# A decoder trunk on one core: operands and weights at one distance modulo 256 bytes, and a few pieces of weights 128 bytes off

## The chip, the cores and the metric

One Trainium2 chip, one of its cores. The metric is the device time of one execution in microseconds (us); a run of the kernel before takes 2272.42 us, the median of three (2271.67 to 2273.33). One further execution was profiled, and its rows are read below.

## What is computed

Two layers of a hybrid decoder on 256 tokens, model width 2048, all float32. Each layer is

```python
h = rms_norm(x, norm1_w)
proj = h @ w_in                                  # 2048 -> 6400
ret = retention(heads(rq), heads(rk), heads(rv), pos)          # 6 heads x 128
att = dilated_attention(heads(aq), heads(ak), heads(av))       # 6 heads x 128
gm  = chunk_gmlp(gu, gv, gmlp_ln_w, gmlp_ws, gmlp_bs)          # 4 groups x 128
mixed = concat(silu(rg) * norm(ret), norm(att), norm(gm))
x = x + mixed @ w_out                            # 2048 -> 2048
x = x + conv_ffn(rms_norm(x, norm2_w), w_up, conv_w, conv_b, w_down)   # 2048 -> 2 * 5632 -> 2048
```

and a last RMS norm follows. Nearly all the work is in the four weight matrices, which are read once each: 792 pieces of 128 x 1024 floats.

## The kernel before

The activations stay in SBUF; the weights come as one stream of pieces, 128 partitions x 1024 floats (4 KB in a partition, 512 KB in all). A piece is loaded into a `raw` buffer by SP, then cut into two float32r tiles: `hi` by ScalarE (line 113) and `lo = raw - hi` by VectorE (line 123), four buffers each. An operand is cut in the same way and lies as one tile of 2 x 256 columns, its high part first: `p0` to `p15` hold the normalised input of a layer half (line 266), `q0` to `q15` what goes into `w_out` (the mixers' outputs) and into `w_down` (the gated up-projection). A product of two floats is then three float32r matmuls of 256 columns: hi by high part, hi by low part, lo by high part. So each piece, eight blocks of 128 x 128, is 24 matmuls, in both forms of the projection:

- `proj_t` (matmul at line 355): the weights are the stationary operand, and `p` or `q` streams past. It does the attention's and the retention's q and k, `w_out`, `w_up` and `w_down`.
- `proj_n` (line 395): here `p` is the stationary operand, and a stretch of `hi` or `lo` streams past. It does the values and gates of the mixers (token major).

By layer the pieces are: attention q and k (24 pieces), attention v (12, `proj_n`), retention q and k (24), then 40 pieces of `proj_n`, `w_out` (32), and three parts of the feed-forward, each `w_up` and then `w_down`: 64 and 32, 64 and 32, 48 and 24. Layer 0 is pieces 0 to 395, layer 1 is 396 to 791.

Between the pieces stand the small matmuls in plain float32: the sums of the norm (lines 310 and 320), the heads of attention and retention (434, 435, 457 to 459, 489, 490, 499 to 501), the gating (554) and the transposes (420, 450). The order is written out by hand: `take` steps the queues of small work (`ev`, `bg`) at each new piece and splits the piece that is three ahead.

Where a tile lies follows from the order of the pools and the tiles' sizes. In the built program the sixteen `p` tiles lie at 192 modulo 256 bytes, and every `hi` and `lo` at 0. The `q` tiles come from `q_tile` (line 412), which makes each one 112 floats longer than its 512 and starts at one of eight places in it:

```python
STARTS = [b // 4 for b in (0, 128, 320, 384, 448, 64, 192, 256)]

def q_tile(slot, which):
    a = STARTS[which]
    return qp.tile([P, 2 * S + 112], F32R, name=f"q{slot}", tag=f"q{slot}")[:, a : a + 2 * S]
```

A `q` tile is therefore 2496 bytes, 9 x 256 + 192, and neighbours lie 192 bytes apart modulo 256: the streaming operand goes round 192, 128, 64 and 0 modulo 256 within every piece of `w_out` and `w_down`. The blocks of one piece start 512 bytes apart, the high and low part of an operand 1024 bytes, so neither changes the place modulo 256. The 128-byte tile `shim` in a pool of its own (line 167, 220) does nothing but move what follows it.

Of the kernel before, what the change touches and what calls it, by code (L numbers as in the profile page):

```python
# [41 lines left out]

PIECE = 1024
PPC = 1
RAW = 4
CHUNK = PIECE * PPC
TOTAL = DEPTH * (D * INW + D * D + D * UPW + DFF * D) // P
NCHUNK = TOTAL // CHUNK
FFN_PARTS = ((0, 16), (16, 32), (32, 44))


# [16 lines left out]
Q_ATT, Q_GM, Q_RET = 0, 6, 10  # L68


class Weights:


    def __init__(self, nc, stream, raw, hp, lp, ahead, step):
        self.nc, self.stream, self.raw, self.hp, self.lp = nc, stream, raw, hp, lp
        self.ahead, self.step = ahead, step
        self.plan = []
        self.pos = 0
        self.loaded = {}
        self.nload = 0  # L80
        self.parts = {}
        self.nsplit = 0
        self.npieces = TOTAL // PIECE

    def load(self, upto):
        while self.nload < min(upto, NCHUNK):
# [16 lines left out]
    def split_hi(self, p, halves=(0, 1)):  # L103
        c = p // PPC
        self.load(c + 1)
        src = self.loaded[c][:, (p % PPC) * PIECE : (p % PPC + 1) * PIECE]
        if p not in self.parts:
            hi = self.hp.tile([P, PIECE], F32R, name=f"hi{p}", tag="hi")
            lo = self.lp.tile([P, PIECE], F32R, name=f"lo{p}", tag="lo")
            self.parts[p] = (hi, lo, src)  # L110
        hi = self.parts[p][0]
        for h in self._halves(p, halves):
            self.nc.scalar.activation(hi[:, h], src[:, h], AF.Copy)  # L113
# [40 lines left out]
def trunk_kernel(tc, x0, xt, stream, par, cst, wst, lnw, out):  # L154
# [5 lines left out]
    with ctx:  # L160
        E = ctx.enter_context

        def pool(name, bufs=1):
            return E(tc.tile_pool(name=name, bufs=bufs))

        cp, xp, pp, qp = pool("cst"), pool("xres"), pool("px"), pool("qx")
        gap = pool("gap")
        wk, fw = pool("mix"), pool("ffn")
        raw, hp, lp = pool("raw", RAW), pool("hi", 4), pool("lo", 4)
        ps = E(tc.tile_pool(name="ps", bufs=4, space=bass.MemoryType.PSUM))  # L170
# [32 lines left out]
        W = Weights(nc, stream, raw, hp, lp, 3, step)  # L203
        live = [0]

        def mm():
            until(lambda: live[0] < 4)
            live[0] += 1
            return ps.tile([P, 512], F32, name="mm", tag="mm")
# [7 lines left out]

        prm = cp.tile([P, NPAR], F32, name="prm")
        warm = cp.tile([P, 2], F32, name="warm")
        shim = gap.tile([P, 32], F32, name="shim")  # L220
        GP.memset(shim, 0.0)
        GP.memset(warm, 0.0)
        A.activation(warm, warm, AF.Copy)
        first = xp.tile([P, NK + 4 * S], F32, name="xg0", tag="xg0")
# [77 lines left out]
        def finish_norm(rot, final=False):  # L302
            while norm["n"] < NK:
                yield
            for _ in range(0 if final else 4 if W.pos < 10 * PIECE else 2):
                yield
            t = mx()
            for j in range(2):
                for i, part in enumerate((norm["acc"], norm["end"])):
                    T.matmul(t[:, j : j + 1], part[:, j * P : (j + 1) * P], ones[:, 0:1], start=i == 0, stop=i == 1)  # L310
            ms = cp.tile([P, 2], F32, name="ms", tag="ms")
            rcol = cp.tile([P, 2], F32, name="rcol", tag="rcol")
            V.tensor_scalar(ms, t[:, 0:2], 1.0 / D, EPS, op0=ALU.mult, op1=ALU.add)
            GP.tensor_tensor(rcol, ms, mhalf[:, 0:2], op=ALU.pow)
            diag = cp.tile([P, S], F32, name="diag", tag="diag")
            for j in range(2):
                V.tensor_scalar(diag[:, j * P : (j + 1) * P], ident, rcol[:, j : j + 1], None, op0=ALU.mult)
            yield
            t = mx()
            T.matmul(t[:, 0:S], ones, diag, start=True, stop=True)  # L320
            if final:
                rbc = t[:, 0:S]
            else:
                rbc = cp.tile([P, S], F32, name="rbc", tag="rbc")
                A.activation(rbc, t[:, 0:S], AF.Copy)
            norm["col"], norm["bc"] = rcol, rbc
            norm["ready"] = True
            if rot:
                for _ in range(12):
                    yield  # L330
                c = wk.tile([P, S], F32, name="cosr", tag="cosr")
                s = wk.tile([P, S], F32, name="sinr", tag="sinr")
# [73 lines left out]
            until(lambda: QX[k] is not None)  # L406
            return QX[k]


        STARTS = [b // 4 for b in (0, 128, 320, 384, 448, 64, 192, 256)]  # L410

        def q_tile(slot, which):
            a = STARTS[which]
            return qp.tile([P, 2 * S + 112], F32R, name=f"q{slot}", tag=f"q{slot}")[:, a : a + 2 * S]

        def mixed_block(slot, l, src, c0):

            t = mx()
            for j in range(2):
                T.transpose(t[:, j * P : (j + 1) * P], src[j][:, c0 : c0 + P], ident)  # L420
            q = q_tile(slot, 4 * l)
            w = prm[:, C_MIX + l * NK + slot : C_MIX + l * NK + slot + 1]
            yield
            split_hi(q, t[:, 0:S], w)
            split_lo(q, t[:, 0:S], w)
            QX[slot] = q


        def attention(h, qk, av, done):
            for _ in range(h if h < WIDTH else 0):  # L430
                yield
            t = mx()
            q, k = qk[h][:, 0:S], qk[h][:, S : 2 * S]
            T.matmul(t[:, 0:P], q[:, 0:P], k[:, 0:P], start=True, stop=True)  # L434
            T.matmul(t[:, P : 3 * P], q[:, P : 2 * P], k, start=True, stop=True)  # L435
            yield
            s = wk.tile([P, 384], F32, name="s", tag="s", bufs=3)
            V.scalar_tensor_tensor(s, t[:, 0:384], SCALE, LC, op0=ALU.mult, op1=ALU.add)
            nm = wk.tile([P, 2], F32, name="nm", tag="nm", bufs=3)
            V.tensor_reduce(nm[:, 0:1], s[:, 0:P], axis=AX.X, op=ALU.max, negate=True)  # L440
            V.tensor_reduce(nm[:, 1:2], s[:, P:384], axis=AX.X, op=ALU.max, negate=True)
            yield
            den = wk.tile([P, 2], F32, name="den", tag="den", bufs=3)
            A.activation(s[:, 0:P], s[:, 0:P], AF.Exp, bias=nm[:, 0:1], accum_out=den[:, 0:1])
            A.activation(s[:, P:384], s[:, P:384], AF.Exp, bias=nm[:, 1:2], accum_out=den[:, 1:2])
            yield
            V.reciprocal(den, den)
            t = mx()
            for i in range(3):
                T.transpose(t[:, i * P : (i + 1) * P], s[:, i * P : (i + 1) * P], ident)  # L450
# [6 lines left out]
            T.matmul(t[:, 0:P], pt[:, 0:P], av[0][:, c], start=True, stop=True)  # L457
            T.matmul(t[:, P : 2 * P], pt[:, P : 2 * P], av[0][:, c], start=True, stop=False)  # L458
            T.matmul(t[:, P : 2 * P], pt[:, 2 * P : 384], av[1][:, c], start=False, stop=True)  # L459
# [26 lines left out]
        def retention(h, qk, rv, scale):  # L486
            t = mx()
            q, k = qk[h][:, 0:S], qk[h][:, S : 2 * S]
            T.matmul(t[:, 0:S], k[:, 0:P], q, start=True, stop=True)  # L489
            T.matmul(t[:, S : S + P], k[:, P : 2 * P], q[:, P : 2 * P], start=True, stop=True)  # L490
# [5 lines left out]
            yield  # L496
            c = slice(h * P, (h + 1) * P)
            t = mx()
            T.matmul(t[:, 0:P], s[:, 0:P], rv[0][:, c], start=True, stop=True)  # L499
            T.matmul(t[:, P : 2 * P], s[:, P : 2 * P], rv[0][:, c], start=True, stop=False)  # L500
            T.matmul(t[:, P : 2 * P], s[:, 2 * P : 384], rv[1][:, c], start=False, stop=True)  # L501
            yield
            for j in range(2):
                V.tensor_copy(rv[j][:, c], t[:, j * P : (j + 1) * P])
# [41 lines left out]
        def gmlp(l, gu, gv, ws, done):  # L546
# [3 lines left out]
            for j in range(2):  # L550
                t = mx()
                for g in range(G):
                    c = slice(g * P, (g + 1) * P)
                    T.matmul(t[:, c], ws[:, c], gv[j][:, c], start=True, stop=True)  # L554
                yield
                for g in range(G):
                    c = slice(g * P, (g + 1) * P)
# [58 lines left out]
        for l in range(DEPTH):  # L616
# [92 lines left out]
            hsn, an = [0], [0]  # L709
            A_TAGS = ("gu0", "gu1", "gv0", "gv1")  # L710

            def up_evac(f0, part):
                gate = {}

                def ev_up(m, acc):
# [16 lines left out]
                        return  # L732
                    V.tensor_tensor(a, a, gate.pop(f), op=ALU.mult)  # L733
                    yield
                    q = q_tile(f - f0, part)
                    A.activation(q[:, 0:S], a, AF.Copy)  # L736
                    yield
                    V.tensor_tensor(q[:, S : 2 * S], a, q[:, 0:S].bitcast(F32), op=ALU.subtract)
# [3 lines left out]
            for i, (f0, f1) in enumerate(FFN_PARTS):  # L742
                last = i == len(FFN_PARTS) - 1
                QX[:] = [None] * NK
                cols = [c for f in range(f0, f1) for c in (f * P, DFF + f * P)]
                proj_t("w_up", l, allrows, cols, p_of, up_evac(f0, 4 * l + 1 + i), 4)
                wcol = None
                if last:
                    PX[:] = [None] * NK
# [100 lines left out]
```

## Time and profile before

| | |
|---|---|
| median of three runs | 2272.42 us |
| the profiled execution | 2269.97 us |
| its span, first to last instruction | 2268.2 us |
| TensorE busy in the span | 2251.2 us, 19430 matmuls |
| VectorE, ScalarE, GpSimd busy | 1443.3, 1143.5, 21.8 us |
| data moved | 425 MB, 187 GB/s on average |
| granted TensorE clock, mean | 0.998 |

The profile counts a matmul as busy from its start to a modelled end, and neighbours overlap, so "99% busy" does not say how fast matmuls follow each other. That is read by dividing a stretch of time by the number of matmuls that start in it. In the view of the chain, which follows the work that ended last, consecutive matmuls of one line are merged into one row with their time and their count, and the quotient stands there directly; a row that begins right behind other matmuls leaves its first one out.

### The profile page before, as it was taken

To read this page: it belongs to the slowest core of one execution; us is meant where nothing else is said; L and a number is where in the kernel's file an instruction comes from. 1 tells how busy PE (TensorE), PEld (TensorE's weight loads), DVE (VectorE), ACT (ScalarE), POOL (GpSimd) and SP (SyncE) were. 2 spreads that over 40 slices of the span, in tenths; PEclk is the share of its full clock that TensorE was granted. 3 is DMA by queue.
4 is the path that set the end of the run, shared out by engine and by line. 5 is a ranking of instruction groups with operands and counts; after the bars stand their busy time and mean duration, and the time that the engine had idled before them with its cause. 6 is when DMAs were issued, how large, how long until landed. Compare 5 with 4: busy or idle time off the path is not lost.

```text
span 2268.2 us, 45995 instructions
## 1 busy us (share of the span) xinstructions
PE 2251.2 (99%) x19430; PEld 2248.1 (99%) x19430; DVE 1443.3 (64%) x2086; ACT 1143.5 (50%) x1616; POOL 21.8 (1%) x39
## 2 busy tenths in 40 slices
PE   9999999999999999999999999999999999999997
PEld 8999999999999999999999999999999999999997
DVE  6565556677547775577655655667775577656765
ACT  6475554555435553455544644555554355434553
POOL 0000000000000000000000001000000000000000
PEclk9999999999999999999999999999999999999999
DMA  8545445555555555565555454555555555555553
GB/s 283 193 158 187 160 168 194 188 194 195 186 186 196 195 182 197 179 206 189 184 201 180 164 180 168 178 184 192 193 192 188 185 199 193 194 186 189 193 191 126
DMA packets 117135, 425.15 MB, mean 187 GB/s; under 512 B 12992, under 2 KB 12992, under 8 KB 116800
## 3 DMA queue, kind: packets, MB, share of 16 engines
q1 hardware_dynamic: 116928, 422.21, 54.8%
q8 instruction: 152, 2.49, 0.4%
q14 instruction: 55, 0.45, 0.1%
HBM read 420.06 MB, written 2.10 MB: 186 GB/s over the span
## 4 chain that ended last, share of the span: by engine, by line
PE 99%; DMA 0%; DVE 0%; SPq 0%; ACT 0%; POOLq 0%; issue 0%; DVEq 0%
PE mm L355 84%; PE mm L395 13%; PE mx L420 0%; DMA xg<-in_xt_dram 0%; PE mx L435 0%; PE mx L489 0%; DVE xg L760 0%; PE mx L310 0%; PE mx L450 0%; PE mx L554 0%; PE mx L458 0%; PE mx L500 0%; PE mx L459 0%; PE mx L501 0%; PE mx L499 0%; PE mx L434 0%
## 5 line engine op out<-in xcount | busy, mean ns | idle before, releaser
L123 DVE TENSOR_TENSOR lo<-raw,hi 128x1024 fp32r<-128x1024 f32 (+1 forms) x793 | 969.0, 1223 | 710.4 <-ACT hi L113 710.2
L113 ACT ACTIVATE hi<-raw 128x1024 fp32r<-128x1024 f32 (+1 forms) x793 | 837.5, 1058 | 881.8 <-PE mm L355 490.7
L355 PE MATMUL mm<-p,hi 128*128 128x256 f32 x7168 | 1235.4, 277 | 5.5 <-ACT hi L113 5.2
L355 PEld LDWEIGHTS mm<-p,hi 128*128 128x128 f32 x7168 | 1084.6, 188 | 6.9 <-ACT hi L113 5.2
L355 PE MATMUL mm<-p,lo 128*128 128x256 f32 x3584 | 991.8, 277 | 0.0
L355 PE MATMUL mm<-q,hi 128*128 128x256 f32 x3840 | 684.8, 281 | 0.0
L355 PEld LDWEIGHTS mm<-p,lo 128*128 128x128 f32 x3584 | 674.3, 188 | 0.5 <-DVE lo L123 0.2
L355 PEld LDWEIGHTS mm<-q,hi 128*128 128x128 f32 x3840 | 589.3, 188 | 0.0
L355 PE MATMUL mm<-q,lo 128*128 128x256 f32 x1920 | 538.4, 280 | 0.0
L355 PEld LDWEIGHTS mm<-q,lo 128*128 128x128 f32 x1920 | 361.6, 188 | 0.0
L395 PE MATMUL mm<-hi,p 128*128 128x256 f32 x1664 | 272.1, 279 | 0.0
L395 PEld LDWEIGHTS mm<-hi,p 128*128 128x128 f32 x1664 | 231.2, 188 | 0.0
L395 PE MATMUL mm<-lo,p 128*128 128x256 f32 x832 | 179.3, 278 | 0.0
L724 ACT ACTIVATE a<-hs,prm 128x256 f32<-128x256 f32 x176 | 104.1, 591 | 63.3 <-DVE hs L369 63.3
L395 PEld LDWEIGHTS mm<-lo,p 128*128 128x128 f32 x832 | 133.3, 188 | 0.0
L727 DVE SCALAR_TENSOR_TENSOR a<-hs,prm,a 128x256 f32<-128x256 f32 x176 | 85.3, 485 | 6.3
L726 DVE SCALAR_TENSOR_TENSOR a<-hs,prm,a 128x256 f32<-128x256 f32 x176 | 84.2, 478 | 4.4 <-ACT a L724 4.4
L692 DVE TENSOR_TENSOR xg<-xg,mm 128x256 f32<-128x256 f32 x128 | 53.3, 418 | 50.7 <-PE mm L355 50.7
L369 DVE TENSOR_TENSOR hs<-mm,rbc 128x256 f32<-128x256 f32 x176 | 73.5, 418 | 2.7 <-PE mm L355 2.7
L730 ACT ACTIVATE a<-a 128x256 f32<-128x256 f32 x88 | 35.6, 405 | 33.5 <-DVE a L727 33.5
L279 ACT ACTIVATE t<-xg 128x256 f32<-128x256 f32 x75 | 30.1, 408 | 39.9 <-DVE xg L692 38.9
L736 ACT ACTIVATE q<-a 128x256 fp32r<-128x256 f32 x88 | 35.4, 403 | 3.5 <-DVE a L733 3.5
(120 smaller groups left out, 578.4 us busy)
## 6 DMA issues: line engine op xcount, KB each, us to landing
raw<-in_stream_dram SPq DMA_DIRECT2D x791, 512.0 KB, 3.4
out_dram<-xg SPq DMA_DIRECT2D x8, 256.0 KB, 2.4
xg<-in_xt_dram SPq DMA_DIRECT2D x3, 512.0 KB, 8.6
cs<-in_cst_dram SPq DMA_DIRECT2D x1, 1216.0 KB, 8.7
raw<-in_stream_dram SPq DMA_DIRECT2D x2, 256.0 KB, 4.2
ws<-in_wst_dram SPq DMA_DIRECT2D x2, 256.0 KB, 4.5
lw<-in_lnw_dram SPq DMA_DIRECT2D x2, 256.0 KB, 4.7
prm<-in_par_dram SPq DMA_DIRECT2D x1, 412.0 KB, 6.0
```

The costliest lines, as they stand in the source:

```text
L113: self.nc.scalar.activation(hi[:, h], src[:, h], AF.Copy)
L123: self.nc.vector.tensor_tensor(lo[:, h], src[:, h], hi[:, h].bitcast(F32), op=ALU.subtract)
L279: A.activation(sq, X[j], AF.Square)
L355: T.matmul(acc[m], w, v, start=k == 0 and i == 0, stop=k == n - 1 and i == 2)
L369: V.tensor_tensor(out, acc, norm["bc"], op=ALU.mult)
L395: T.matmul(acc[j][:, c], v, w[:, c], start=k == 0 and i == 0 and c.start == 0, stop=k == NK - 1 and i == 2, skip_group_check=True)
L692: V.tensor_tensor(X[m], X[m], acc, op=ALU.add)
L724: A.activation(a, hs[:, 2 : S + 2], AF.Identity, scale=conv_col(ch, 2), bias=conv_col(ch, 3))
L726: V.scalar_tensor_tensor(a, hs[:, 1 : S + 1], conv_col(ch, 1), a, op0=ALU.mult, op1=ALU.add)
L727: V.scalar_tensor_tensor(a, hs[:, 0:S], conv_col(ch, 0), a, op0=ALU.mult, op1=ALU.add)
L730: A.activation(a, a, AF.Silu)
L736: A.activation(q[:, 0:S], a, AF.Copy)
```

## The change

It touches where tiles lie, and nothing of what is computed. Four things change:

1. `q_tile` with its eight starts is gone, and with it the padding: a `q` tile has 512 floats, 2048 bytes, as a `p` tile has. So all `q` tiles lie at 192 modulo 256, where the `p` tiles lie.
2. `hi` and `lo` tiles get 64 floats more (`SLACK`), and a piece starts 32 floats into them if it goes to `proj_t` and 0 floats if it goes to `proj_n` (`PLACES`, `token_major`). With `shim` removed the tiles' own start moves as well: in the built program a piece of `proj_t` lies at 0 modulo 256, 192 bytes before its operand, and a piece of `proj_n` at 128, which is 192 past the operand at 192 (before: at 0, which is 64 past it).
3. Every small float32 matmul and transpose sets a mark (`stirred`). The next piece that gets its buffers then starts at the other of the two places and clears the mark, if at least four pieces (`APART`) have gone since the last such one. Its distance is then 64 bytes and not 192. In the built program these are 40 pieces, 20 in each layer: 10, 14, 39, 43, 47, 51, 55, 59, 63, 75, 79, 83, 87, 91, 95, 99, 103, 107, 137 and 141 in layer 0; 401, 405, and then 396 past those from 39 on in layer 1.
4. There are five `raw` buffers in place of four.

```diff
-RAW = 4
+RAW = 5
+SLACK = 64
+PLACES = ((32, 0), (0, 32))
+APART = 4
...
+def token_major(p):
+    p %= LAYER_PIECES
+    a, b = QK_PIECES + AV_PIECES, 2 * QK_PIECES + AV_PIECES
+    return QK_PIECES <= p < a or b <= p < b + REST_PIECES
...
+    def place(self, p):
+        other = self.stirred and p - self.moved >= APART
+        if other:
+            self.stirred, self.moved = False, p
+        a = PLACES[token_major(p)][other]
+        return slice(a, a + PIECE)
...
         if p not in self.parts:
-            hi = self.hp.tile([P, PIECE], F32R, name=f"hi{p}", tag="hi")
-            lo = self.lp.tile([P, PIECE], F32R, name=f"lo{p}", tag="lo")
-            self.parts[p] = (hi, lo, src)
+            at = self.place(p)
+            hi = self.hp.tile([P, PIECE + SLACK], F32R, name=f"hi{p}", tag="hi")
+            lo = self.lp.tile([P, PIECE + SLACK], F32R, name=f"lo{p}", tag="lo")
+            self.parts[p] = (hi[:, at], lo[:, at], src)
...
+        def matmul(*args, **kw):
+            W.stirred = True
+            T.matmul(*args, **kw)
+
+        def transpose(*args):
+            W.stirred = True
+            T.transpose(*args)
...
-        shim = gap.tile([P, 32], F32, name="shim")
-        GP.memset(shim, 0.0)
...
-            q = q_tile(slot, 4 * l)
+            q = qp.tile([P, 2 * S], F32R, name=f"q{slot}", tag=f"q{slot}")
...
-                    q = q_tile(f - f0, part)
+                    q = qp.tile([P, 2 * S], F32R, name=f"q{f - f0}", tag=f"q{f - f0}")
```

All the small matmuls and transposes now go through `matmul` and `transpose`, so a profile of the changed kernel shows them under the lines of these two helpers.

TensorE, ScalarE and VectorE get the same instructions in the same order as before, and GpSimd loses the fill of `shim`. What moves is on SP, by the fifth buffer. At the start of the program (the rows carry the tile that is loaded, its number, and the events that the load waits for), the loads of the weights stood so:

```order
L232 DMA xg3_99<-in_xt_dram 128x1024 [waits DMAHW1_49]
L89 DMA raw4_211<-in_stream_dram 128x1024 [waits DMAHW3_49,DMAHW2_49,DVE_49]
L89 DMA raw5_213<-in_stream_dram 128x1024 [waits DMAHW5_49,DVE_49]
L89 DMA raw6_215<-in_stream_dram 128x1024 [waits DMAHW6_49,DMAHW4_49,DVE_49]
L89 DMA raw7_221<-in_stream_dram 128x1024 [waits DMAHW7_49,DVE_49]
```

and now:

```order
L265 DMA xg3_94<-in_xt_dram 128x1024 [waits DMAHW1_49]
L115 DMA raw4_206<-in_stream_dram 128x1024 [waits DMAHW2_49]
L115 DMA raw5_208<-in_stream_dram 128x1024 [waits DMAHW3_49,DVE_49]
L115 DMA raw6_210<-in_stream_dram 128x1024 [waits DMAHW5_49,DMAHW4_49,DVE_49]
L115 DMA raw7_212<-in_stream_dram 128x1024 [waits DMAHW6_49,DVE_49]
```

The load of piece 4 no longer waits for VectorE, which had to be done with piece 0 in the same buffer; each later one waits for a split that comes one piece earlier. A little further on, the tables (`cs`: masks and rotation; `prm`: scales and convolution) stood among the loads so:

```order
L89 DMA raw13_465<-in_stream_dram 128x1024
L597 DMA cs_114<-in_cst_dram 128x2432
L89 DMA raw14_514<-in_stream_dram 128x1024
L89 DMA raw15_520<-in_stream_dram 128x1024
L89 DMA raw16_554<-in_stream_dram 128x1024
L600 DMA prm_90<-in_par_dram 128x824
```

and now:

```order
L115 DMA raw14_462<-in_stream_dram 128x1024
L623 DMA cs_109<-in_cst_dram 128x2432
L115 DMA raw15_511<-in_stream_dram 128x1024
L115 DMA raw16_517<-in_stream_dram 128x1024
L115 DMA raw17_551<-in_stream_dram 128x1024
L626 DMA prm_87<-in_par_dram 128x824
```

Each table stands behind one more load of weights than before.

## Rows read from the trace of the kernel before

**Rows 1.** The page: busy time by engine; the chain's shares by line.

```profile
PE 2251.2 (99%) x19430; PEld 2248.1 (99%) x19430; DVE 1443.3 (64%) x2086; ACT 1143.5 (50%) x1616; POOL 21.8 (1%) x39
...
PE mm L355 84%; PE mm L395 13%; PE mx L420 0%; DMA xg<-in_xt_dram 0%; PE mx L435 0%; PE mx L489 0%; DVE xg L760 0%; PE mx L310 0%; PE mx L450 0%; PE mx L554 0%; PE mx L458 0%; PE mx L500 0%; PE mx L459 0%; PE mx L501 0%; PE mx L499 0%; PE mx L434 0%
```

**Rows 2.** Stretches, TensorE: length, busy time (matmuls), granted clock, DMA share, GB/s.

```profile
322.31:402.10 79.79, 79.79 (x674) 1.00 0.54 183
414.44:577.64 163.20, 163.20 (x1442) 1.00 0.56 192
577.64:668.95 91.31, 91.31 (x770) 1.00 0.56 189
668.95:843.06 174.11, 174.11 (x1538) 1.00 0.57 192
843.06:933.98 90.92, 90.92 (x771) 1.00 0.56 189
...
1064.54:1133.06 68.52, 68.52 (x578) 1.00 0.55 191
1444.96:1524.52 79.56, 79.56 (x675) 1.00 0.54 182
...
1700.05:1790.96 90.91, 90.91 (x770) 1.00 0.55 190
...
1965.05:2055.97 90.92, 90.92 (x770) 1.00 0.57 190
...
2186.53:2254.93 68.40, 68.40 (x578) 1.00 0.43 146
```

**Rows 3.** The chain from 60 to 330: start, length, engine and line, instructions.

```profile
77.28 32.64 PE mm L395 x288
...
110.57 2.74 PE mm L355 x24
...
113.96 2.84 PE mm L355 x24
...
187.32 32.64 PE mm L395 x288
...
229.58 14.14 PE mm L395 x120
...
304.50 5.66 PE mm L395 x48
```

**Rows 4.** The chain of the whole span: around the norm between the layers.

```profile
1139.47 2.93 PE mm L355 x24
1142.40 0.43 PE mx L320 x2
1142.83 57.14 PE mm L355 x504
```

**Rows 5.** Instructions in order, TensorE: the end of `w_down`, the start of `w_up`.

```profile
933.62 0.40 PE L355 MATMUL mm<-q,hi 128*128 128x256 f32 x2
...
933.98 0.40 PE L355 MATMUL mm<-p,hi 128*128 128x256 f32 x2
...
934.32 0.39 PE L355 MATMUL mm<-p,hi 128*128 128x256 f32 x2
934.55 0.28 PE L355 MATMUL mm<-p,lo 128*128 128x256 f32 x1
```

**Rows 6.** The page: the splits' busy and idle time; then loads, last us to landing.

```profile
L113 ACT ACTIVATE hi<-raw 128x1024 fp32r<-128x1024 f32 (+1 forms) x793 | 837.5, 1058 | 881.8 <-PE mm L355 490.7
...
raw<-in_stream_dram SPq DMA_DIRECT2D x791, 512.0 KB, 3.4
```

**Rows 7.** The table `cs`: its first reader, and its load (min/median/max, first and last start).

```profile
L333 DVE TENSOR_TENSOR cosr<-cs,rbc x2: 419/420/420, 68.6 to 1175.0; 128x256 f32<-128x256 f32 x2
...
L597 SPq DMA_DIRECT2D cs<-in_cst_dram x1: 426/426/426, 32.2 to 32.2; - x1
```

More of the change, by code (lines that the diff above doesn't have):

```diff
@@ L48 @@
 NCHUNK = TOTAL // CHUNK
+SLACK = 64
+PLACES = ((32, 0), (0, 32))
+LAYER_PIECES = TOTAL // PIECE // DEPTH
+QK_PIECES = 2 * H * D // PIECE
+AV_PIECES = H * D // PIECE
+REST_PIECES = (2 * H + 2 * G) * D // PIECE
+APART = 4
 FFN_PARTS = ((0, 16), (16, 32), (32, 44))
@@ L83, in __init__ @@
         self.npieces = TOTAL // PIECE
+        self.stirred = False
+        self.moved = 0
+    def place(self, p):
[4 more added lines that the diff above has]
+        return slice(a, a + PIECE)
     def load(self, upto):
@@ L166, in trunk_kernel @@
         cp, xp, pp, qp = pool("cst"), pool("xres"), pool("px"), pool("qx")
-        gap = pool("gap")
         wk, fw = pool("mix"), pool("ffn")
@@ L309, in finish_norm @@
                 for i, part in enumerate((norm["acc"], norm["end"])):
-                    T.matmul(t[:, j : j + 1], part[:, j * P : (j + 1) * P], ones[:, 0:1], start=i == 0, stop=i == 1)
+                    matmul(t[:, j : j + 1], part[:, j * P : (j + 1) * P], ones[:, 0:1], start=i == 0, stop=i == 1)
             ms = cp.tile([P, 2], F32, name="ms", tag="ms")
@@ L319, in finish_norm @@
             t = mx()
-            T.matmul(t[:, 0:S], ones, diag, start=True, stop=True)
+            matmul(t[:, 0:S], ones, diag, start=True, stop=True)
             if final:
@@ L407, in q_of @@
             return QX[k]
[L410 to L414, printed above, removed]
         def mixed_block(slot, l, src, c0):
@@ L419, in mixed_block @@
             for j in range(2):
-                T.transpose(t[:, j * P : (j + 1) * P], src[j][:, c0 : c0 + P], ident)
-            q = q_tile(slot, 4 * l)
+                transpose(t[:, j * P : (j + 1) * P], src[j][:, c0 : c0 + P], ident)
+            q = qp.tile([P, 2 * S], F32R, name=f"q{slot}", tag=f"q{slot}")
             w = prm[:, C_MIX + l * NK + slot : C_MIX + l * NK + slot + 1]
@@ L433, in attention @@
             q, k = qk[h][:, 0:S], qk[h][:, S : 2 * S]
-            T.matmul(t[:, 0:P], q[:, 0:P], k[:, 0:P], start=True, stop=True)
-            T.matmul(t[:, P : 3 * P], q[:, P : 2 * P], k, start=True, stop=True)
+            matmul(t[:, 0:P], q[:, 0:P], k[:, 0:P], start=True, stop=True)
+            matmul(t[:, P : 3 * P], q[:, P : 2 * P], k, start=True, stop=True)
             yield
@@ L449, in attention @@
             for i in range(3):
-                T.transpose(t[:, i * P : (i + 1) * P], s[:, i * P : (i + 1) * P], ident)
+                transpose(t[:, i * P : (i + 1) * P], s[:, i * P : (i + 1) * P], ident)
             yield
@@ L456, in attention @@
             t = mx()
-            T.matmul(t[:, 0:P], pt[:, 0:P], av[0][:, c], start=True, stop=True)
-            T.matmul(t[:, P : 2 * P], pt[:, P : 2 * P], av[0][:, c], start=True, stop=False)
-            T.matmul(t[:, P : 2 * P], pt[:, 2 * P : 384], av[1][:, c], start=False, stop=True)
+            matmul(t[:, 0:P], pt[:, 0:P], av[0][:, c], start=True, stop=True)
+            matmul(t[:, P : 2 * P], pt[:, P : 2 * P], av[0][:, c], start=True, stop=False)
+            matmul(t[:, P : 2 * P], pt[:, 2 * P : 384], av[1][:, c], start=False, stop=True)
             yield
@@ L488, in retention @@
             q, k = qk[h][:, 0:S], qk[h][:, S : 2 * S]
-            T.matmul(t[:, 0:S], k[:, 0:P], q, start=True, stop=True)
-            T.matmul(t[:, S : S + P], k[:, P : 2 * P], q[:, P : 2 * P], start=True, stop=True)
+            matmul(t[:, 0:S], k[:, 0:P], q, start=True, stop=True)
+            matmul(t[:, S : S + P], k[:, P : 2 * P], q[:, P : 2 * P], start=True, stop=True)
             yield
@@ L498, in retention @@
             t = mx()
-            T.matmul(t[:, 0:P], s[:, 0:P], rv[0][:, c], start=True, stop=True)
-            T.matmul(t[:, P : 2 * P], s[:, P : 2 * P], rv[0][:, c], start=True, stop=False)
-            T.matmul(t[:, P : 2 * P], s[:, 2 * P : 384], rv[1][:, c], start=False, stop=True)
+            matmul(t[:, 0:P], s[:, 0:P], rv[0][:, c], start=True, stop=True)
+            matmul(t[:, P : 2 * P], s[:, P : 2 * P], rv[0][:, c], start=True, stop=False)
+            matmul(t[:, P : 2 * P], s[:, 2 * P : 384], rv[1][:, c], start=False, stop=True)
             yield
@@ L553, in gmlp @@
                     c = slice(g * P, (g + 1) * P)
-                    T.matmul(t[:, c], ws[:, c], gv[j][:, c], start=True, stop=True)
+                    matmul(t[:, c], ws[:, c], gv[j][:, c], start=True, stop=True)
                 yield
@@ L710, in trunk_kernel, with up_evac @@
             A_TAGS = ("gu0", "gu1", "gv0", "gv1")
-            def up_evac(f0, part):
+            def up_evac(f0):
                 gate = {}
@@ L745, in trunk_kernel @@
                 cols = [c for f in range(f0, f1) for c in (f * P, DFF + f * P)]
-                proj_t("w_up", l, allrows, cols, p_of, up_evac(f0, 4 * l + 1 + i), 4)
+                proj_t("w_up", l, allrows, cols, p_of, up_evac(f0), 4)
                 wcol = None
```

## The prediction, made before the changed kernel ran

> **What bounds the kernel now.** First the page: TensorE is busy 99% of the span, and the chain of work that ended last lies with 84% on line 355 and 13% on line 395, the two projections [rows 1]. Everything else is beside them, so only what changes the spacing of those matmuls can change the time by much. Busy time hides the spacing; the next view is therefore stretches of single stages, each cut at the start of its first matmul. A stretch counts one to three matmuls too many, those that reach over its ends; the real number is pieces times 24.
>
> In `w_up` the 60 pieces from 414.44 take 163.20 us for 1440 matmuls, 113.33 ns each, and the 64 from 668.95 take 174.11 for 1536, 113.35. The `w_down` between them, from 577.64, takes 91.31 for 768: 118.89. The others: 90.92, 90.91 and 90.92 for 768 each (118.4), 68.52 and 68.40 for 576 (119.0 and 118.8). `w_out` without its first four pieces: 79.79 and 79.56 for 672 (118.7 and 118.4) [rows 2]. The same instruction, the same clock of 1.00, the same share of DMA, and 5.3 ns apart. What differs is the place of the streaming operand: `p` always at 192 past the weights modulo 256, `q` going round four places.
>
> The third view, the chain, shows that the place is not all. With `p` as operand throughout, a piece behind attention's float32 matmuls runs 24 matmuls in 2.74 us (114) or in 2.84 (118). In `proj_n` the first 288 take 32.64 (113.3), twice; behind the retention's matmuls 120 take 14.14 (117.83), and this stays so up to 48 in 5.66 at 304.50: ten such stretches, 28 pieces in each layer [rows 3]. So at one distance there are two paces, 113.33 and 117.83, and small float32 work can put TensorE from the first into the second. It also comes back: behind the norm's line 310 a piece takes 2.93 us, and behind line 320 the next 504 take 57.14, 113.4 [rows 4]. I call these fast and slow. One piece at the slow pace costs 24 x 4.50 = 0.108 us.
>
> **The other views that bear on this change.** Coming from the mixed places onto `p` ended fast all seven times: the two long `w_up` stretches of rows 2 begin right behind `w_out` or `w_down`. In two of the seven the last `q` stood at 64, the distance of the moved pieces: there three matmuls at 64 start 0.36 us before the next three, and from 934.32 the step is down to about 0.34 [rows 5]. This is the nearest row for what a moved piece does.
>
> **The change part by part.** All sums are against the profiled execution, 2269.97 us with a span of 2268.2; it is 2.45 under the median of the runs, to which I add the result at the end.
>
> *`q` at 192 in `w_down`.* The operands then lie as `p` lies in the `w_up` before, with no float32 work between, so the pace is carried over. The six stretches sum to 500.98 us for 4224 matmuls [rows 2]; at 113.33 they take 478.71. Gain 22.27.
>
> *`q` at 192 in `w_out`.* The two stretches of 28 pieces sum to 159.35 for 1344 [rows 2]; fast they take 152.32, gain 7.03. It begins behind transposes, so it needs the moved piece just before it (103, 499) to leave it fast. A moved piece (107, 503) lies in each, slow by my estimate below: 0.22. Net 6.82. The first four pieces I leave as they are.
>
> *The moved pieces themselves.* The trace has whole pieces at 64 only in `proj_n`: fast at 32.64 for 288, slow at 14.14 for 120 [rows 3]. In the mixed `w_down` the three matmuls at 64 take 0.36 [rows 5], so about slow. From 0 to 0.108 us each; I take 0.108, since the row at line 355 is nearer to them than `proj_n`.
>
> *`proj_n`, now at 192.* Of the 28 slow pieces of a layer I count fast only those between a moved piece and the next float32 work: 76 to 78, 80, 84, 85, 88, 92 to 94 and 96, eleven. Piece 63, fast now, becomes a moved one. Net ten pieces, 1.08 us a layer, 2.16 in all.
>
> *Retention's q and k.* Pieces 47, 51 and 59 are fast and get moved, 39 is half; 56 becomes fast. Net 0.27 a layer, a loss of 0.54. The heads' `q` and `k` tiles move to 192 as well. The piece behind a head that already lay there takes 2.74 us (at 110.57), that behind the next head 2.84 (at 113.96) [rows 3]; this could give three pieces a layer. I leave that gain of up to 0.65 to the range.
>
> *Moved pieces in fast stretches.* 10 and 14, 137 and 141, and the same four in layer 1: 8 x 0.108 = 0.86 lost.
>
> *The fifth `raw` buffer.* A load lands in 3.4 us, and the split on ScalarE is idle 490.7 us waiting for TensorE to free a `hi` buffer [rows 6]: weights are never late, so deeper loading gains nothing behind the start. On SP, `cs` is now behind one more load. It is issued at 32.2 and first read at 68.6 [rows 7]; 3.4 later is still early. `prm` is behind one load more as well, and is read later still. The load of piece 4 no longer waits for VectorE and may run beside the last loads of `x`; that delays the start by anything from 0 to the 3.4 of one load. I take 0, since pieces 1 to 3 go ahead of it already, and keep 3.4 for the range. If this cover went, ScalarE's split would be late first and the matmuls at line 355 behind it.
>
> *Removed fill of `shim`, wider tiles.* GpSimd is busy 21.8 us of the span [rows 1], and the splits process as many elements as before. Nothing.
>
> The sum: 22.27 + 6.82 + 2.16 - 0.54 - 0.86 = 29.85. The profiled execution would be 2240.1, and the median 2272.42 - 29.85 = **2242.6 us**. A measurement of this kernel tells about 0.2%, 4.5 us, from no change.
>
> **A rule that speaks against it.** The rows say that the spacing follows the operand's place [rows 2]. The Trainium skill says otherwise: its page "TensorE: Matmul & The Clock Gate", section "Step-by-step: what each phase is for", gives TensorE two independent read ports to SBUF, one for the streaming operand and one for the weights, and says that loading the next weights takes no read bandwidth from the running matmul. By that rule the sum is 0 and the time 2272.4. The trace differs: 118.89 against 113.33 ns.
>
> **The rivals.**
>
> *A: places do not matter (4%).* Something else that `w_out` and `w_down` share sets their pace, such as the residual adds or the order of `q`. For it: the trace has no long run of `q` at 192. Against it: `proj_n` slows to almost the same pace with `p`, and with none of that work. Gain 0, or the small losses above: 2272 to 2274.
>
> *B: a moved piece does not restore the fast pace (13%).* Then `w_out` runs slow at 117.83, 158.36 for the two stretches, a gain of 0.99; `proj_n` gains nothing and loses piece 63, 0.22; retention loses three moved pieces a layer, 0.65, and the fast stretches 0.86. With `w_down`, which does not depend on it, 22.27 + 0.99 - 0.22 - 0.65 - 0.86 = 21.53: **2250.9**. For it: 64 to 192 shows only behind three matmuls at 64, with the operand moved and not the weights.
>
> *C: moved pieces end in the slow pace (7%), slower than before.* The place is behind 137 and 141: from there to the end of the layer some 258 pieces have no float32 work that could put it right. In each layer these, about 25 behind 10 and 14, 12 behind 59, the 27 of `w_out` and the 11 of `proj_n` would cost 0.108 more than forecast: 333 x 0.108 = 36.0, in both 71.9, so **2314**. It decides when some 276 pieces that I count at 113.33 ns take 117.83 (29.85 / 0.108); a single bad landing behind 141 costs 27.9 and all but eats the gain. Against it: seven fast landings of seven.
>
> *D: at 192 `proj_n` finds back by itself, and moved pieces are as fast as the others (15%).* For it: at line 355, at 192, pieces behind float32 work are often fast; at line 395, at 64, none of the ten stretches is. Then 38 moved pieces that I charge cost nothing (4.1), nine unmoved pieces a layer of `proj_n` turn fast (1.9), and the heads give 0.65: **2236**.
>
> **How the numbers follow.** My forecast has 61%, D 15%, B 13%, C 7%, A 4%. The range goes from D's 2236 to B's 2251; inside it lies the 3.4 of a late start. It leaves out C and A. Faster by over 0.2%: forecast, B, D and the mildest of C, 0.90. Within 0.2%: A and a C with one bad landing, 0.04. Slower: 0.06.
>
> **What would show it.** In the changed profile, stretches of `w_down` at 113.3 ns a matmul, 87.04 us for 32 pieces, show the first term; anything near 118 is A. `w_out` behind piece 107 at 113.3 shows that a moved piece restores, 117.8 is B. A `w_up` behind piece 141 at 117.8 is C. A moved piece takes 2.83 us if I price it rightly, 2.72 in D. The first matmul at 5.2 us as before, and ScalarE still waiting for TensorE, show that the fifth buffer is neutral. I am wrong if `w_down` is not uniform, or if its pace depends on more than the distance modulo 256.

## The result and the profile after

The changed kernel takes 2241.84 us (median of four runs, 2241.59 to 2242.37); the kernel before, run beside it on that chip, 2272.05 (2270.55 to 2273.33). The ratio is 0.9868 with a 95% interval of 0.985 to 0.9885: faster, by more than the 0.2% that can be told. On another chip the two stood at 2242.03 and 2270.09, a ratio of 0.9876 (0.9861 to 0.9891). The forecast was 2242.6 with a range of 2236 to 2251.

The profiled executions are 2269.97 us before and 2242.37 after, 27.6 apart, against a forecast of 29.85. That the forecast of the median came within 0.8 is in part luck: the runs of before that it started from lay some 2 us above those of the other chip, where the gain is 28.06.

The page of the changed kernel, its busy time, the chain's shares, the splits and the loads:

```profile
PE 2223.4 (99%) x19430; PEld 2220.2 (99%) x19430; DVE 1443.3 (64%) x2086; ACT 1143.9 (51%) x1616; POOL 24.4 (1%) x38
...
PE mm L388 84%; PE mm L428 13%; PE mx L235 2%; PE mx L239 0%; DMA xg<-in_xt_dram 0%; DVE xg L786 0%; SPq L125 0%; SPq L261 0%; POOLq L870 0%; DVEq L870 0%; ACT p L290 0%; DVE diag L350 0%; DVE xg L718 0%; ACT t L312 0%; DVE ms L346 0%
...
L140 ACT ACTIVATE hi<-raw 128x1024 fp32r<-128x1024 f32 (+1 forms) x793 | 837.4, 1058 | 851.3 <-PE mm L388 459.5
...
raw<-in_stream_dram SPq DMA_DIRECT2D x791, 512.0 KB, 3.8
```

Against [rows 1] and [rows 6] nothing has changed places: the same 19430 matmuls, TensorE at 99%, the chain with 84 and 13% on the two projections (now lines 388 and 428), the split still waiting for TensorE. TensorE's busy time fell by 27.8 us: the same work is spaced more tightly. So the stretches again, cut at the first matmul of a stage as in [rows 2] (length, busy time and matmuls, granted clock, DMA share, GB/s). In the order shown: the moved piece 103; pieces 104 to 106; the moved piece 107; 108 to 131; then `w_up` and `w_down` in turn, and three stretches of layer 1.

```profile
320.04:322.96 2.92, 2.92 (x28) 1.00 0.52 180
322.96:331.12 8.16, 8.16 (x75) 1.00 0.45 152
331.12:333.84 2.72, 2.72 (x27) 1.00 0.34 133
333.84:399.12 65.28, 65.28 (x579) 1.00 0.59 197
...
411.45:574.65 163.20, 163.20 (x1442) 1.00 0.60 192
574.65:661.69 87.04, 87.04 (x771) 1.00 0.58 198
661.69:835.77 174.08, 174.08 (x1539) 1.00 0.57 192
835.77:922.81 87.04, 87.04 (x771) 1.00 0.58 199
...
1053.37:1118.65 65.28, 65.28 (x579) 1.00 0.58 200
...
1431.10:1507.26 76.16, 76.16 (x674) 1.00 0.56 189
1682.80:1769.83 87.03, 87.03 (x770) 1.00 0.57 198
```

`w_down` takes 87.04 us for 768 matmuls, 113.33 ns each, exactly the number that the prediction asked for; `w_out` from piece 104 on takes 8.16 + 2.72 + 65.28 = 76.16 for 28 pieces, 113.33 too. A moved piece inside a stretch of the fast pace (107) takes 2.72, no more than its neighbours. The clock is 1.00 and the DMA share what it was.

The chain from 60 to 420 (start, length, engine and line, instructions) shows what was lost:

```profile
77.40 33.92 PE mm L428 x288
111.32 0.66 PE mx L235 x4
111.98 2.74 PE mm L388 x24
114.71 0.66 PE mx L235 x4
115.37 2.74 PE mm L388 x24
...
134.95 1.32 PE mx L235 x10
136.28 2.82 PE mm L388 x24
...
188.50 33.08 PE mm L428 x288
...
231.21 13.73 PE mm L428 x120
...
253.80 14.14 PE mm L428 x120
...
296.30 5.66 PE mm L428 x48
...
320.29 84.43 PE mm L388 x744
404.72 0.79 PE mx L235 x8
405.51 2.93 PE mm L388 x24
408.44 0.43 PE mx L235 x2
```

In [rows 3] the first 288 matmuls of `proj_n` took 32.64, twice. Now the first such stretch takes 33.92, 117.8 ns each, and the second 33.08: pieces 60 to 63 are slow in it. Nothing in the prediction allowed for that. The piece behind a head that was slow at 113.96 in [rows 3] now takes 2.74 (at 115.37).

### The profile page after: what moved, and what is told of

Same layout as the page of the kernel before. It is cut to its first block, busy times and chain, and to the rows that moved or that the text cites. A ratio compares the mean times of both kernels' runs of the same rounds, so it can differ in the third digit from the quotient of the medians.

```text
span 2240.6 us, 45994 instructions
## 1 busy us (share of the span) xinstructions
PE 2223.4 (99%) x19430; PEld 2220.2 (99%) x19430; DVE 1443.3 (64%) x2086; ACT 1143.9 (51%) x1616; POOL 24.4 (1%) x38
## 4 chain that ended last, share of the span: by engine, by line
PE 99%; DMA 0%; DVE 0%; SPq 0%; ACT 0%; POOLq 0%; issue 0%; DVEq 0%
PE mm L388 84%; PE mm L428 13%; PE mx L235 2%; PE mx L239 0%; DMA xg<-in_xt_dram 0%; DVE xg L786 0%; SPq L125 0%; SPq L261 0%; POOLq L870 0%; DVEq L870 0%; ACT p L290 0%; DVE diag L350 0%; DVE xg L718 0%; ACT t L312 0%; DVE ms L346 0%
## 5 line engine op out<-in xcount | busy, mean ns | idle before, releaser
L140 ACT ACTIVATE hi<-raw 128x1024 fp32r<-128x1024 f32 (+1 forms) x793 | 837.4, 1058 | 851.3 <-PE mm L388 459.5
L388 PE MATMUL mm<-q,hi 128*128 128x256 f32 x3840 | 655.2, 276 | 0.0
L388 PEld LDWEIGHTS mm<-q,hi 128*128 128x128 f32 x3840 | 578.6, 188 | 0.0
L388 PE MATMUL mm<-q,lo 128*128 128x256 f32 x1920 | 530.1, 276 | 0.0
```

The costliest lines, as they stand in the source:

```text
L388: T.matmul(acc[m], w, v, start=k == 0 and i == 0, stop=k == n - 1 and i == 2)
```

## The experiments

Two questions stood: which of the forecast's terms carried the gain, and what made 2.25 us less of it. The theory: distance sets the paces, a moved piece restores the fast one, and `proj_n` at 192 loses at its first piece. The rivals: moved pieces do nothing here, the places themselves do all (or: distance does not matter, only the order of the work). A border is the change from one form of the projection to the other; a landing is the step from a moved piece back to the usual distance. Every kernel here computes all that the reference does; only addresses and the number of buffers differ. Times are medians; where there is one run its time stands.

**1. No moved pieces.**

```diff
-        a = PLACES[token_major(p)][other]
+        a = PLACES[token_major(p)][0]
```

> The changed kernel with no piece moved: every piece of weights stays at its usual place, 192 from its operand. Theory (TensorE has two paces, 113.3 and 117.8 ns a matmul; float32 work can put it into the slow one, and a step of the distance from 64 to 192 takes it back): w_out runs at 117.8 from its first pieces to the norm's matmuls, 85.5 us for 30 pieces against 81.6 now, pieces 64 to 71 and 460 to 467 stay slow (0.86 us a layer), and so do 76 to 78, 80 and 88 and their like; w_down keeps 113.3. Together 4.7 us a layer, about 2251.8. Rival (the distance alone sets the pace, the moved pieces are idle): no stage changes, 2242.4.

Measured: 2242.66 us (2241.19 to 2243.16), ratio 0.9878 (0.9863 to 0.9893). The rival's number, but not its reason: the stages did change, and what they lost and won cancels. The chain of this kernel:

```profile
76.72 33.92 PE mm L428 x288
...
187.65 33.92 PE mm L428 x288
...
231.20 13.62 PE mm L428 x120
...
296.16 5.46 PE mm L428 x48
...
319.75 84.35 PE mm L388 x744
```

`w_out` runs at 113.4 ns (84.35 for 744) with no moved piece in it: piece 103 left the transposes ahead of it in the fast pace. The second 288 of `proj_n` are slow throughout, 33.92 against 33.08 after; this is what the moved piece 63 had bought, pieces 64 to 71. Piece 80 was bought as well. The moves cost as much: pieces 40, 55, 75, 87, 95, 96, 97, 99 and 103 are fast here and slow in the changed kernel (74 to 78 take 13.62 here and 13.73 there, 95 and 96 take 5.46 and 5.66). That is nine pieces a layer against nine, so that the sum stays is luck.

**2. `proj_n` at 64 again, moved pieces kept.**

```diff
-PLACES = ((32, 0), (0, 32))
+PLACES = ((32, 0), (32, 0))
```

> The changed kernel with the two places of proj_n exchanged: the usual distance is 64 again, as in the kernel before, and a moved piece is at 192. Theory (the twelve pieces of attention's v and the first of the gates are slow now because the border from proj_t to proj_n at 192 puts TensorE into the slow pace, and at 64 it does not): pieces 24 to 35 and 60 to 62 run at 113.3 again, 1.28 + 0.32 us a layer, so about 2239.2, if a step from 192 back to 64 restores as often as one from 64 to 192 does now. If that step never restores, five later pieces a layer turn slow, 0.54: 2240.3. Rival (the slow start of proj_n has another cause, such as the wider tiles or the fifth buffer): 24 to 35 stay at 117.8 and the time stays at 2242.4.

Measured: 2241.53 us (2241.33 to 2241.9), ratio 0.9874 (0.9857 to 0.989). The chain:

```profile
77.75 32.64 PE mm L428 x288
...
187.57 33.60 PE mm L428 x288
```

The first 288 are back at 113.3, so `proj_n`'s new distance is what made its beginning slow, and not the wider tiles or the fifth buffer. The second lost 0.96: the moved piece 63, at 192 among pieces at 64, is slow itself, and the pieces behind it stay slow. Landings from 192 on 64 spoil there: three a layer were entered fast, and the piece behind was slow each time (80, 84 and 96). With pieces 63 to 71 slow and these landings, the time lies above both of the theory's numbers, 2239.2 and 2240.3.

**3. `q` at 192 alone: `proj_n` at 64, no moved pieces.**

```diff
-        a = PLACES[token_major(p)][other]
+        a = 32
```

> The q tiles at 192 and nothing else: no piece moved, proj_n at 64 as in the kernel before. Theory: w_down 113.3 in all six stretches, pieces 24 to 35 and 60 to 71 at 113.3 as in the kernel before, the 28 pieces of proj_n behind the retention at 117.8, w_out at 117.8 up to the norm: about 2247, so about five sixths of the gain. Rival (the moved pieces bring nothing, and proj_n at 64 is better than at 192): at or under 2242.

Measured: 2245.88 us (2244.97 to 2249.13), ratio 0.9896 (0.9881 to 0.991). The theory's number, about 1 under it. The chain:

```profile
77.05 32.64 PE mm L428 x288
...
318.52 87.63 PE mm L388 x744
```

Here `w_out` runs at 117.8 ns from end to end, 3.2 us lost a layer, though its own operands lie exactly as in experiment 1. The two kernels differ in the distance of `proj_n` alone, so what ran before `w_out` decides.

**4. Four `raw` buffers.**

```diff
-RAW = 5
+RAW = 4
```

> The changed kernel with four raw buffers. Theory (weights are never late): the time of the changed kernel within 0.5 us, 2242; the first two pieces within 0.4 us of the kernel before. Rival (five buffers carry part of the gain): over 2244, with waits of ScalarE's split for loads.

Measured: 2243.95 us in one run. The time is 2 over the theory's and just under the rival's; the split waits once for a load, 0.8 us (once, 0.4, in the changed kernel). Every stage behind the first has the excess of the changed kernel, to 0.01 us (the excess is defined in the next section); the 1.68 lies ahead of `proj_n`:

```profile
2.66 6.45 DMA xg<-in_xt_dram
...
9.69 24.41 PE mm L388 x180
...
79.08 33.92 PE mm L428 x288
```

In the changed kernel these rows read 5.86, 23.33 and a start at 77.40. Of the 1.68, 0.64 is the pace of pieces 2 to 7, which run at 117.8 here. They do so too in the second execution of the changed kernel, which has five buffers and starts `proj_n` at 78.17. The first load of `x` took from 5.28 to 7.04 us with five buffers (experiments 1 and 5) and 5.70 in experiment 8 with four. `proj_n` starts at 77.28 before (four buffers), at 77.13 in experiment 8 (four) and at 78.47 in experiment 5 (five). The start varies by as much, and one run does not settle what the fifth buffer is worth.

**5. `proj_n` at 64 where it is entered from `proj_t`, at 192 behind float32 work; moved pieces in `proj_t` alone.**

```diff
+def early(p):
+    p %= LAYER_PIECES
+    return p < QK_PIECES + AV_PIECES or 2 * QK_PIECES + AV_PIECES <= p < 2 * QK_PIECES + 2 * AV_PIECES
...
+        if token_major(p):
+            a = 32 if early(p) else 0
+            return slice(a, a + PIECE)
```

> proj_n at 64 for the 24 pieces of a layer that follow proj_t without float32 work (24 to 35, 60 to 71), at 192 for the 28 behind the retention, no moved piece in proj_n; proj_t moved as in the changed kernel. Theory (a border from proj_t keeps the pace at 64 and loses it at 192; behind float32 work 192 finds back now and then, 64 almost never): the 24 run at 113.3 (2.72 us a piece), the 28 as in the run without moved pieces (about 1.6 us a layer over 113.3), w_out fast from the piece behind the moved one: about 2237.5, 4 to 5 below the changed kernel. Rival (the paces behind float32 work are a toss that any shift throws anew): the 24 fast, the 28 anything from all slow to half fast, 2236 to 2240.

Measured: 2238.42 us (2237.3 to 2240.23), ratio 0.9855 (0.9836 to 0.9874). With moved pieces in `proj_t` alone, those of `w_out` fall on 100, 104 and 108 in place of 103 and 107. It was run again beside the changed kernel on one chip:

> The kernel with two distances in proj_n once more, beside the changed kernel on one chip: 2238, 3 to 5 below the changed kernel. Rival (the difference was one of chips): under 1 apart.

> The changed kernel once more, for the comparison: 2242, excesses over 113.3 by stage as in its first profile.

Measured: 2238.58 (2238.09 to 2238.99), ratio 0.986 (0.9844 to 0.9877), against 2242.03 (2241.2 to 2242.62) of the changed kernel; before took 2270.09. The chain in the second execution:

```profile
78.10 32.64 PE mm L436 x288
...
187.92 32.64 PE mm L436 x288
...
222.52 5.46 PE mm L436 x48
229.98 14.13 PE mm L436 x120
```

Both long stretches are at 113.3. This is the best version found: 3.45 us under the changed kernel, 31.5 under the one before. 1.28 us a layer come from the first stretch, 0.65 from the later ones. The late pieces are not as in experiment 1, as the theory had them: 72 and 73 are fast here and slow there, 74 to 78 slow here and fast there (5.46 at 222.52 and 14.13 at 229.98, against 13.62). For these pieces the rival, that any shift throws the paces anew, is not excluded, and its range holds the time too.

**6 and 7. Every piece of `proj_t` at 0, or at 128** (`proj_n` at 64).

```diff
-        a = PLACES[token_major(p)][other]
+        a = 32 if token_major(p) else 16
```

> Every piece of proj_t at distance 0 from its operand, p and q alike; proj_n at 64, no moved piece; to be read against the run with q alone, where proj_t is at 192. Theory A (any one distance will do; what cost w_down its pace was the change of place within a piece): w_up and w_down at 113.3, 2246 give or take the stretches behind float32 work (2243 to 2252). Theory B (192 is a distance that runs fast, 0 is not): w_up and w_down at 117 to 119, over 2300.

Measured: 2350.51 us in one run. With 48 in the place of 16:

> The same at distance 128. Theory A: 113.3 in w_up and w_down, 2243 to 2252. Theory B: 117 to 120, over 2300.

Measured: 2331.12 us. `w_down` and the `w_up` behind it, at distance 0 first:

```profile
595.98:688.14 92.16, 92.16 (x770) 1.00 0.57 186
688.14:872.46 184.32, 184.32 (x1538) 1.00 0.54 182
```

and at 128:

```profile
593.73:684.86 91.13, 91.13 (x770) 1.00 0.56 188
684.86:867.14 182.28, 182.28 (x1539) 1.00 0.55 184
```

92.16 / 768 is 120.0 ns, 91.13 / 768 is 118.7, in both matrices alike, and from piece 2 on no piece of `proj_t` runs at 113.3 at either distance, whatever stands ahead of it.

**8. `q` at 64, the rest of `proj_t` at 192** (`proj_n` at 64, no moved pieces, four `raw` buffers).

```diff
-        a = PLACES[token_major(p)][other]
+        a = 32
...
-            q = qp.tile([P, 2 * S], F32R, name=f"q{slot}", tag=f"q{slot}")
+            q = qp.tile([P, 2 * S + 64], F32R, name=f"q{slot}", tag=f"q{slot}")[:, 32 : 32 + 2 * S]
```

The `q` of `w_down` is shifted in the same way.

> p at 192 and all q at 64 past the weights, one place each; no moved piece, proj_n at 64, four raw buffers. Theory A (one distance within a stage will do, and a border keeps the pace, as the moved pieces at 64 did): w_down at 113.3, about 2246. Theory B (in the kernel before, three matmuls with an operand at 64 were slow at once behind a fast w_up, so a step of the operand's place loses the pace): w_down at 117.8 from its first matmuls, back to 113.3 in the w_up behind it; 176 pieces at 0.108 us, about 2265.

Measured: 2264.18 us in one run. `w_up`, `w_down`, `w_up`, `w_down`:

```profile
412.87:576.07 163.20, 163.20 (x1443) 1.00 0.59 192
576.07:666.52 90.45, 90.45 (x771) 1.00 0.57 191
666.52:840.61 174.09, 174.09 (x1539) 1.00 0.58 192
840.61:931.06 90.45, 90.45 (x771) 1.00 0.58 191
```

Each `w_down` takes 90.45, 117.8 ns, six of six, and each `w_up` behind one is back at 113.3. So a step of the operand from 192 to 64 loses the fast pace, and the step from 64 to 192 finds it.

**9. Every piece of `proj_t` at 64** (`proj_n` at 64).

```diff
-        a = PLACES[token_major(p)][other]
+        a = 32 if token_major(p) else 0
```

> Every piece of proj_t at distance 64, p and q alike; proj_n at 64, no moved piece. Theory (64 has the same two paces as 192, 113.3 and 117.8, but hardly ever finds back from the slow one by itself): the first pieces at 113.3, and from the first float32 work behind piece 7 nearly everything at 117.8, in w_up and w_down too: some 680 pieces at 0.107 us over a time of 2232 without any, and 5 for proj_n: about 2310. Rival (64 is as good as 192 once it is uniform): w_up and w_down at 113.3, 2243 to 2250.

Measured: 2314.84 us in one run. `w_down` and `w_up`:

```profile
589.23:679.68 90.45, 90.45 (x770) 1.00 0.58 190
679.68:860.59 180.91, 180.91 (x1539) 1.00 0.56 185
```

117.8 ns nearly everywhere, from the first pieces of the program on, which the theory had at 113.3. The fast pace exists here too: piece 102, between transposes, has its matmuls 113.3 apart. But the norm, behind which every kernel at 192 is fast again, does not bring it back.

**10. Experiment 3 with the moved pieces in `proj_t` put back.**

```diff
+        if token_major(p):
+            return slice(32, 32 + PIECE)
```

> The run with q alone (proj_n at 64, nothing moved there) with moved pieces in proj_t alone. Theory (a step from 64 back to 192 restores the fast pace in proj_t): w_out, which ran at 117.8 there, 3.2 us a layer over 113.3, runs at 113.3 from the piece behind the first moved one, 0.2 to 0.4 over; the rest as there: about 2240, 6 under the run with q alone. Rival (w_out is a toss of the float32 work before it, and a moved piece does not change it): 2246, or the toss falls well with no moved piece just ahead of the change of pace.

Measured: 2239.31 us (2238.77 to 2240.24), ratio 0.9865 (0.985 to 0.9879). The chain:

```profile
318.59 84.53 PE mm L390 x744
```

Where `w_out` is entered slow, a moved piece turns it: 84.53 against 87.63 in experiment 3. Piece 104, the moved one, is still slow and 105 is fast, in both layers. In the whole program the moves are worth some 6 us here: 6.6 by the medians, which come from two chips (before took 2270.21 and 2270.09), 6.1 by the profiled executions, 5.8 of it in `w_out`. In the changed kernel nothing can be told: `w_out` would find the fast pace without them, and elsewhere they win and lose the same number of pieces (experiment 1).

## Why the prediction was right, and where its steps were off

To set the terms beside what came, the starts of all matmuls in the two projections were taken from the trace, and what their spacing has over 113.33 ns was summed by stage, leaving out waits at the start and the first matmul behind float32 work. Before, this excess is 38.46 us; after, 10.22.

```
term of the sum                        forecast   measured
q at 192 in w_down                       22.27      22.28   (22.28 before, 0.00 after)
w_out                                     6.82       7.41   (8.05 before, 0.64 after)
proj_n at 192                             2.16      -1.88   (5.92 before, 7.80 after)
retention q and k, heads                 -0.54       0.40   (1.60 before, 1.20 after)
moved pieces in fast stretches           -0.86       0.03   (0.55 before, 0.52 after)
sum                                      29.85      28.24
```

The forecast of `w_out` left its first four pieces out. The 28 behind them gave 7.03, the fast pace throughout; the other 0.38 came from the first four. The misses partly cancel: `proj_n` fell 4.04 short, and the other rows came out 2.43 above their forecast.

The rest of the difference to 27.6 is the start (the third piece begins 0.28 later), and 0.53 in the last norm, to within 0.2. The last norm's two matmuls of 256 columns, before and after:

```profile
2258.57 0.68 PE mx L320 x2
2230.44 1.21 PE mx L235 x2
```

The granted clock there was 1.00 before and 0.50 (1.2 GHz) after. In the profiled execution of the changed kernel it fell at 2229.5, after the projections had ended and six one-column matmuls had run; in the second execution it fell only behind the two matmuls, and they took 0.68 again. So the same kernel shows both, and the 0.53 is not put down to the change.

**The first term held to 0.01 us.** `w_down` carries the fast pace of `w_up`, all six times. That was three quarters of the forecast, and experiment 8 is its counterproof: the same `w_down` with `q` at 64 costs 90.45 in place of 87.04.

**Rival A, that places do not matter, is out.** The same instruction at a clock of 1.00 takes 113.33 ns at 192 in `w_up` and `w_down`, 117.8 at 64, 118.7 at 128 and 120.0 at 0, by nothing but the address. The Trainium skill ("TensorE: Matmul & The Clock Gate", section "Step-by-step: what each phase is for") says that loading the next weights takes no read bandwidth from the running matmul; by that rule the four kernels that differ in the distance of `proj_t` alone would take the same time. At 192, 64, 128 and 0 (experiments 3, 9, 7 and 6) they took 2245.88, 2314.84, 2331.12 and 2350.51 us, and the measurement decides.

**The step "`w_out` needs the moved piece just before it" failed as a reason, though its size held.** Without moved pieces `w_out` enters the fast pace by itself (experiment 1). With `proj_n` at 64 it does not (experiment 3), and then the moved piece does what the forecast said (experiment 10, and four landings of four in the changed kernel's `proj_t`: behind 55, 103, 451 and 499). So rival B falls, and the half of D that says that 192 finds back by itself was right for `w_out`, in this company.

**The term "moved pieces", 0.108 us each, was mis-sized.** I took the price of the slow pace from three mixed matmuls in `w_down`. Within a mixed piece that price cannot be read: in the `w_down` of before the starts of two neighbours at 192 lie 119.6 apart on average, at 64 117.8, at 128 120.3 and at 0 117.8, which is not the order of the uniform kernels. In whole pieces of `proj_t` a moved one keeps the pace in which it is entered, where no float32 work stands ahead of it: 107, 137, 141 and the like take 2.72, so the price is 0, as D said. Eight such pieces and the two in `w_out` were charged 1.08 us for nothing. Rival C is out by the same pieces: behind 137 and 141 all of `w_up` runs at 113.33.

**The term "`proj_n`, now at 192" failed: 4.04 us short.** I counted landings alone and took 192 for no worse than 64 where `proj_n` is entered. But coming straight from `proj_t`, with no float32 work between, the fast pace was lost at 192 in four borders of four (two a layer; experiment 1 also four of four), and kept at 64 in every kernel that enters from the fast pace (experiments 2, 3, 5, 8 and 10). That is 12 pieces behind the first border and four behind the second (60 to 63, of which 63 was in the forecast as a moved piece), 1.73 us a layer. Of the landings, eight of 14 restored: behind 63, 75, 79 and 87, not behind 83, 91 and 95; so of the eleven pieces that I counted five came, and the five pieces of 84, 85 and 92 to 94 did not, nor did 96. Pieces 74, 86 and 98 came back by themselves, some 0.3 us a layer that was not forecast.

**The retention's term had the wrong sign** because heads at 192 now return in the fast pace (2.74 at 115.37), the gain that I had left to the range, and because the moved pieces 47, 51 and 59 cost nothing. Pieces 39 and 40, at 114.1 and 113.6 before, are slow after and take 0.2 a layer of it back.

**The fifth buffer and the rest**: the load lands in 3.8 us instead of 3.4 and the split still waits for TensorE, 459.5 us. Nothing to be told, as forecast; the start varies by more (experiment 4, one run).

What stays open: why the border from `proj_t` to `proj_n` loses the fast pace at 192 and not at 64, and why three of seven landings in `proj_n` fail. Other distances for the late pieces of `proj_n`, and landings with the stationary operand there, were not tried.

## What to carry to other kernels

When one matmul's spacing differs between stages at the same clock, cut stretches by stage and set the address of the streaming operand against that of the weights beside them: bringing the mixed operand to the best distance (here 192 modulo 256) was worth 1.0% by itself (experiment 3), in a kernel whose TensorE was already 99% busy. Choose the distance for each form of matmul and for each border between forms by itself, and forecast a moved operand from how a border was entered, not from its distance alone. A repair such as a moved piece is worth only what the place would not find by itself: measure it with and without, in the final company of the other changes.

## What the runs showed of the hardware that was not expected

**Four distances, four paces.** 113.33 or 117.8 at 192 and at 64 (two paces each), 118.7 at 128, 120.0 at 0, all at a clock of 1.00. The figures at 128 and 0 are of one run each.

**It matters which operand moves.** In `proj_t`, going from 192 to 64 by moving the weights keeps the fast pace (14 steps of 14 in the changed kernel). Going there by moving the streaming operand loses it: six of six in experiment 8, and six of six in `proj_n` in the changed kernel, where the pieces are the streaming side. Both are counted where the step was entered fast and no float32 work stood at it. Going from 64 back to 192 in `proj_t` turned slow into fast in every case, four of four in the changed kernel and seven of seven in experiment 8. In `proj_n` the step from 64 to 192 does so only in part: eight of 14 landings in the changed kernel, four of ten moved pieces entered slow in experiment 2, and there it also lost the fast pace two times of two (piece 63).

**The pace behind small float32 work follows a pattern.** In `proj_t` at 192 on both sides, counted over the traces of the changed kernel and experiments 1, 2, 3, 5, 8 and 10: behind 4 float32 matmuls (as the chain counts them) the next piece is fast, from either pace, 48 of 48; behind 6 it is fast, 42 of 42, all entered fast; behind 8 or 10 it is slow, 34 of 34. The chain of the changed kernel above shows one of each: 2.74 behind `x4` at 114.71, 2.82 behind `x10` at 134.95. Behind the norm's 8 the piece is slow (2.93 at 405.51), behind its last 2 fast. Two transposes ahead of piece 103 swapped the pace: from slow to fast in experiments 1 and 5, from fast to slow in 3 and 10. So the pace of `w_out` in these kernels goes back to the pace ahead of the transposes. The number of matmuls is not the cause by itself, for the kinds of work differ with it. In the kernel before, the same 4 leave pieces 37, 38 and 45 slow (2.84 at 113.96 in [rows 3]) and 36 and 44 fast: in the built program the heads' tiles lie at 128 or 64 modulo 256 ahead of the first three and at 192 ahead of the other two. And not everything is in the pattern: behind three transposes piece 39 is slow in experiment 1 and fast in experiment 3, in both layers, with the same places and the same pace ahead. All this was read from the traces afterwards and not tested by a kernel of its own.
